# Sending ScalarE's transfers through SyncE, with longer portions of other work ahead of the gate chain's last two steps

## The chip, the cores and the metric

The kernel runs on one core of a Trainium2 chip. The metric is device time in microseconds (us). The kernel before has a median of 1401.21 us over 3 runs (1399.54 to 1405.23).

## The reference

It is one step of a two-layer trunk with 128 context tokens and 512 latent tokens of 1024 features, all in float32. Each layer normalises and modulates its input and projects it once; three branches read that projection: A, latent attention; B, differential attention; C, an mLSTM in both directions. Each branch is multiplied by its own gate path, one output projection follows, and a gated residual is added. Cut to what matters here:

```python
def mixer_layer(x, mod, l, W, rope, ctx):
    shift, scale, gate = jnp.split(mod, 3, axis=-1)
    h = rmsnorm(x, W['g_norm'][l]) * (1 + scale) + shift
    proj = h @ W['W_in'][l]
    ...
    gts = (mg + W['ml_gate_b'][l].reshape(N_ML_GATES)).astype(f32)      # input and forget gates, per token
    ...                                                                 # lf = log_sigmoid(forget), cumulated per chunk
    m_t = jnp.maximum(g, jnp.max(d, axis=-1))                           # running-max stabiliser of the scan
    ...
    y = jnp.concatenate([o_a * jax.nn.silu(z_a), o_b * jax.nn.silu(z_b), o_c * jax.nn.silu(z_c)]) @ W['W_out'][l]
    return x + gate * y, side
```

The outputs are both residual streams after a final norm and, for the context tokens, the keys, values and mLSTM states of each layer.

## The kernel before

All 640 tokens are held together as five tiles of 128. Every projection is made from three float32r products per 128 features (`mm3`, L287 to L290), because weights and activations are split in a high and a low part. A token-major unit (`tm_unit`, L478) takes 24 such matmuls of up to 256 columns per token tile; a feature-major unit (`fm_unit`, L467) takes 24 matmuls of 320 columns per half of the tokens.

Weights come through `load_w` (L263): SyncE issues the load into one of three raw slots (L278; L275 for four-dimensional sources), ScalarE casts it to the high part (L279), and VectorE or every third time GpSimd subtracts to get the low part (L282). There are five slots each for the high and the low parts.

Two mechanisms set the order of the work.

The first is written by hand. `Feed` (L80) holds the independent units of a layer in the order `ORDER` (L133): va0 qk0 mo0 zc0 qk1 gt0 and so on. A dependent chain is a generator which yields a number of us after each of its steps; `along` (L117) hands that number to `pull` (L107), which adds it to a debt and emits units while the debt is above zero, each unit taking its own number off (2.6 for a token tile, 3.2 for a feature-major half). `need` (L113) emits all that stands ahead of a named unit at once, without touching the debt.

The second is the framework's planner. It keeps the program's order as a priority, but in each engine's queue it puts what its own estimate says is ready first. Each queue is then executed in that order: an instruction whose inputs are not there holds up everything behind it on its engine. An issue of a transfer is an instruction of its engine's queue like any other.

The gate chain (`gates`, L621) stands at the head of each layer's work, after the values va0. It transposes the gate pre-activations, forms the log-sigmoid, cumulates it per chunk (L643, L644), runs the max scans (L651 to L657) and adds (L660). It then sends the stabilisers to DRAM (L663) and the prompt's final ones to the output (L665, L666), and yields 6.4. The next step takes the chunk ends (L671 to L678), forms the factors (L681 to L686), and yields 3. The last step broadcasts those factors by a matmul (`abp`, L690), transposes the result of L678 (`pa`, L696) and the stabilisers (`pb`, L697), and copies them out as columns (L700 to L702). The first mLSTM head follows (`mlstm_head`, L707): it reloads the stabilisers on all partitions (`mb`, L715), transposes keys (`pk`, L724), weights them (`kw`, L727), and computes `pst` (L732) and the state updates `cu` (L737).

Transfers that ScalarE issues in this kernel are: the stabilisers and two small outputs (L663 to L666, eight in all), the bias row of each residual gate (L369, eight) and the gate row to DRAM (L371, eight; L377 reads it back on all partitions), the new residual after a part of the output projection (L540, 60), the same in the last head of the first layer (L562, 10), and the final gain (L1217, 2). All others are issued by SyncE.

In `out_proj` (L522) a token tile's old residual is loaded (L531), VectorE multiplies the product by the gate (L538), GpSimd adds (L539) and ScalarE issues the store (L540). The gate rows (`grw`, L368) come from a ring of eight slots (`et`, L175), which also serves the exponentials of the mLSTM head (L755, L762) and its state outputs (L748). Other lines named below: L581 copies the values va out of PSUM; L595 does the same with a tanh for the output gates mo; L828 copies transposed probabilities out of PSUM; L1028 and L1030 split the latent keys; L813 and L816 split the keys of branch B; L849 and L867 store its values and keys.

Of the kernel before, what the change touches and what calls it, by code (L numbers as in the profile page):

```python
# [32 lines left out]
# columns of the constant array  # L33
C_ID, C_SEL, C_BLK, C_ONE, C_PRM, C_RC, C_RS, C_MF, C_END = (
    0, 128, 130, 138, 266, 436, 692, 948, 1204)
# columns of the parameters among them
# [29 lines left out]
def parameter_columns(I):  # L66
    """Vectors of the inputs laid out as columns of 128, and the gate biases and stabilisers on their gate rows."""
    names = ("c", "c_ctx", "g_norm", "mla_q_norm", "mla_kv_norm", "diff_norm", "ml_conv", "ml_norm",
             "state_mlstm_n", "b_mod")
    c = np.zeros((P, C_RC - C_PRM), np.float32)  # L70
    c[:, 0:R_GB] = np.concatenate([I[n].reshape(-1, P) for n in names]).T
    for d in range(2):
        for ty in range(2):
            q0 = ty * 64 + d * 32
            c[q0:q0 + H, R_GB:R_GB + DEPTH] = I["ml_gate_b"][:, d, ty, :].T
        c[d * 32:d * 32 + H, R_M0:R_M0 + DEPTH] = I["state_mlstm_m"][0, :, d, :].T
    return c


class Feed:  # L80
    """Independent work, emitted in portions between the steps of a dependent chain."""
# [41 lines left out]
def tile_hybrid(ctx: ExitStack, tc: tile.TileContext, I: dict, O: dict):  # L123
# [8 lines left out]
    # independent work of a layer, in the order in which it fills the gaps of the dependent chains  # L132
# [7 lines left out]
    class Fixed:  # L140
        """One tile from which all that stays in its place is cut."""
# [14 lines left out]
    class Ring:  # L156
        """Slots used in turn, for tiles that live for a short stretch of the program."""
# [32 lines left out]
    # ---------------------------------------------------------------- constants and parameters  # L190
# [12 lines left out]
    # silu(cond) as stationary columns: [c_hi, ctx_hi, c_lo, ctx_lo] per k  # L203
# [13 lines left out]
    # half conv weights; norm gains with the half of z's silu  # L217
# [29 lines left out]
    # ---------------------------------------------------------------- helpers  # L247
    def rsq(ss, n, mul, eps=EPS):
        """1/sqrt(ss*mul + eps) on [P, n] columns."""
        a, r = st("rqa"), st("rqr")  # L250
        V.tensor_scalar(a[:, :n], ss, mul, eps, op0=ALU.mult, op1=ALU.add)  # L251
        G.tensor_tensor(r[:, :n], a[:, :n], mhalf[:, :n], op=ALU.pow)  # L252
        return r[:, :n]
# [9 lines left out]
    def load_w(parts, kt, w, pool=3):  # L263
        """Streams a weight section; returns per-k views of its exact high and low parts."""
# [27 lines left out]
    # ---------------------------------------------------------------- modulation  # L292
# [4 lines left out]
    def mod_rows(l, c0, pool):  # L297
        ps = pj("modp")
        if pool is None:
            # before there is other work for the tensor engine: unsplit  # L300
# [34 lines left out]
    def mod_col(l, part, s, res, pool=3):  # L335
        """Columns [P, k, which] of two feature tiles of the shift or of the scale."""
# [13 lines left out]
    def mod_end(l, res, k=slice(0, 8)):  # L350
        """(1 + scale) * g and shift."""
# [11 lines left out]
    def mod_gate(l, s, pool=3):  # L363
# [5 lines left out]
        A.dma_start(out=row[0:2, :], in_=I["b_mod"][l, 2048 + s * 256:2304 + s * 256].unsqueeze(0).to_broadcast([2, 256]))  # L369
        V.tensor_tensor(row[0:2, :], ps[0:2, 0:256], row[0:2, :], op=ALU.add)  # L370
        A.dma_start(out=grow[l][:, s * 256:(s + 1) * 256], in_=row[0:2, :])  # L371

    def gate_tile(l, hf):
        """The residual gates of half of the features for the sample and for the prompt, on all partitions."""
# [5 lines left out]
    # ---------------------------------------------------------------- residual stream  # L380
# [48 lines left out]
    def norm_sample(s, xs, mods, hT):  # L429
        """Two feature tiles of the normalised sample: transposed, modulated and split."""  # L430
# [8 lines left out]
    def norm_prompt(s, xs, mods, hT):  # L439
        """Four feature tiles of the normalised prompt."""  # L440
# [16 lines left out]
    # ---------------------------------------------------------------- projections  # L457
# [9 lines left out]
    def fm_unit(hT, wv, c0, cb):  # L467
        """Feature-major unit of 128 columns: cb(half, psum of 320 tokens)."""
# [9 lines left out]
    def tm_unit(hT, wv, w, cb):  # L478
        """Token-major unit: cb(token tile, psum [P, w])."""
# [8 lines left out]
    def z_sec(l, hT, key, c0, res, h):  # L488
        """2 * silu(z) of a head, feature-major."""
# [10 lines left out]
    def head_norm(tok, sq, mul):  # L500
        """rmsnorm over the 128 features of each of the 5 token tiles; in place."""
# [7 lines left out]
    def finish(tok, tmp, gcol, z):  # L509
        """Token-major head output -> gated, feature-major, split in high and low."""  # L510
# [11 lines left out]
    def out_proj(l, br, ks, res, key, v):  # L522
        """x += gate * (heads ks of a branch) @ W_out, for all tokens."""
        for hf in range(2):
# [3 lines left out]
            for t in range(NT):  # L528
# [11 lines left out]
                A.dma_start(out=xd[v][t][:, cs], in_=xt)  # L540
                yield 0.65 * len(ks)

    def out_tail(l, br, ks, res, key, v):
        """The last heads of a layer, token tile by token tile; gives the new residual tiles."""
# [3 lines left out]
        def tile_(t):  # L548
            w = 0 if t < 4 else 1
            xs = x_tiles(v - 1, t)  # L550
            for hf in range(2):
# [9 lines left out]
                if l + 1 < DEPTH:  # L561
                    A.dma_start(out=xd[v][t][:, cs], in_=xs[hf])  # L562
# [3 lines left out]
    # ---------------------------------------------------------------- branch C: mLSTM  # L566
    def sec_va(l, hT, p, res):
        """Values of a pair of heads (and the gates with the first pair), token-major."""
# [35 lines left out]
    def conv_unit(l, hT, wv, c0, ch, res, key):  # L604
        """Depthwise conv and silu, feature-major."""
# [15 lines left out]
    def gates(l, res):  # L621
# [40 lines left out]
        for d in range(2):  # L662
            A.dma_start(out=msc[d * 4:d * 4 + 4, :], in_=m[d * 32:d * 32 + 4, :])  # L663
        # final stabilisers of the prompt
        A.dma_start(out=O["new_mlstm_m"][0, l, 0, :].unsqueeze(1), in_=mt[0:4, 639:640])  # L665
        A.dma_start(out=O["new_mlstm_m"][0, l, 1, :].unsqueeze(1), in_=mt[32:36, 512:513])  # L666
        yield 6.4
# [20 lines left out]
        yield 3  # L688
# [18 lines left out]
    def mlstm_head(l, h, res, feed, nfin):  # L707
# [8 lines left out]
        # value of [C | n] at the start of each chunk  # L716
# [33 lines left out]
        for c in range(NT):  # L750
            if c < 4:
                # q scaled by the weight of the incoming state
# [34 lines left out]
    # ---------------------------------------------------------------- attention pieces  # L787
    def rope(dst, x, t, s, on=None):
        """dst, x: [P, s*64] of sample token tile t."""
# [9 lines left out]
    def q_stack(ps, r0, n):  # L799
        """rows r0..r0+64 of ps -> [q_hi; q_lo], for each of r0."""  # L800
# [7 lines left out]
    def k_stack(ps, parts):  # L808
        """(r0, n0, kh, kl): rows r0..r0+64 of ps from column n0 -> [k_hi; k_hi], [k_lo; k_lo]."""
# [11 lines left out]
    def attend(pe, t, v3, vp, hs):  # L821
        """psum [q, dv] = P @ V, P token-major."""
# [12 lines left out]
    # ---------------------------------------------------------------- branch B: differential attention  # L835
    def sec_dv(l, hT, p, res):
        """Values of a pair of heads: sample | context cache, and prompt."""
# [16 lines left out]
    def sec_dqk(l, hT, h, res):  # L854
        """q | k of a head, token-major, rotated; the context cache as fifth key tile."""
# [100 lines left out]
    # ---------------------------------------------------------------- branch A: latent attention  # L956
# [24 lines left out]
    def mla_prep(l, res):  # L981
        ch = [*res["cq", 0], *res["cq", 1], res["cq", 2][0]]
        kr3 = res["cq", 2][1]
        # per-token norms of cq and ckv
# [16 lines left out]
        # prompt outputs  # L1001
# [8 lines left out]
        # transposed, with the gain; split  # L1010
# [4 lines left out]
        for k in range(2):  # L1015
            # columns: sample | context cache | prompt
# [29 lines left out]
        # shared rotary key: sample (rotated) | context cache | prompt  # L1046
# [13 lines left out]
        # rotary queries, token-major over all heads  # L1060
# [21 lines left out]
    def mla_v(l, p, res):  # L1082
        """Values of a pair of heads, token-major: sample | context cache, and prompt."""
# [17 lines left out]
    def mla_qk(l, h, res):  # L1101
        """Queries and keys of a head without the rotary part, feature-major, split."""
# [30 lines left out]
    def mla_head(l, h, res, feed, tail=None):  # L1133
# [45 lines left out]
        # the last head: every token tile goes on to the end of the layer by itself  # L1179
# [30 lines left out]
    # ---------------------------------------------------------------- the trunk  # L1210
    gfin = [None]

    def final_norm(t, xs):
        if gfin[0] is None:
            gfin[0] = [qt("gfin", n=512) for _ in range(2)]
            for i in range(2):
                A.dma_start(out=gfin[0][i],  # L1217
# [147 lines left out]
```

## Time and profile before

| what | value |
|---|---|
| median of 3 runs | 1401.21 us |
| runs | 1399.54, 1401.21, 1405.23 us |
| span of the profiled execution | 1399.6 us |
| PE busy | 1310.0 us, 94% |
| VectorE busy | 842.5 us, 60% |
| ScalarE busy | 630.2 us, 45% |
| GpSimd busy | 385.5 us, 28% |
| mean granted TensorE clock | 0.977 |

The span runs from the first to the last instruction. Of the profiled execution no other time is shown, so the span stands for it; it is 1.6 us below the median of the runs and equals the fastest of them. PE is TensorE's matmuls, PEld its weight loads, DVE VectorE, ACT ScalarE, POOL GpSimd. SPq and ACTq are the queues of SyncE and ScalarE when they issue transfers. A granted clock of 1.00 is 2.4 GHz, 0.50 is 1.2 GHz.

### The profile page before, as it was taken

The page shows a single profiled execution, that of the slowest core. Times are in us where ns is not written, and L with a number is a line of the kernel's source. Part 1 is how long each engine was busy: PE and PEld are TensorE (multiplying, and loading weights), DVE is VectorE, ACT ScalarE, POOL GpSimd, SP SyncE. Part 2 cuts the span into 40 slices and gives each one's busy share as a digit, 9 for nine tenths or more (in the row PEclk, how much of TensorE's full clock was granted, in tenths as well). Part 3 has the DMA queues.
Part 4 walks back from the last instruction along what each step waited for, and adds up shares of the span by engine and source line. Part 5 has one row for each costly group of instructions (what it writes and reads, how often), then busy time and mean ns, then how long its engine had stood idle before and what let it go on. Part 6 is the DMA issues. An engine that isn't in the chain of part 4 may idle for free.

```text
span 1399.6 us, 24039 instructions
## 1 busy us (share of the span) xinstructions
PE 1310.0 (94%) x9300; PEld 1218.9 (87%) x9300; DVE 842.5 (60%) x1786; ACT 630.2 (45%) x1333; POOL 385.5 (28%) x335
## 2 busy tenths in 40 slices
PE   8989999989899999999979899999999999899995
PEld 3789899969899999798769899998799999878984
DVE  2576757765567465854465767675655646385446
ACT  5454544433455545255365345443343445435433
POOL 0421422323223013511432213333322202161142
PEclk9999999999999999999989999999999999999998
DMA  9423323264223223531751333434521211242154
GB/s 341 116 83 101 111 84 112 85 212 136 81 83 111 61 62 113 167 109 54 238 176 31 84 112 86 117 82 129 180 84 57 74 46 63 87 138 85 54 173 150
DMA packets 164642, 156.40 MB, mean 112 GB/s; under 512 B 14193, under 2 KB 130593, under 8 KB 164529
## 3 DMA queue, kind: packets, MB, share of 16 engines
q1 hardware_dynamic: 154032, 135.92, 32.0%
q10 hardware_dynamic: 10496, 18.95, 3.6%
q8 instruction: 73, 1.20, 0.3%
q14 instruction: 41, 0.33, 0.1%
HBM read 131.38 MB, written 23.46 MB: 111 GB/s over the span
## 4 chain that ended last, share of the span: by engine, by line
PE 73%; DVE 12%; DMA 5%; ACT 4%; issue 2%; POOL 2%; SPq 1%; DVEq 0%; ACTq 0%; POOLq 0%
PE tm L288 8%; PE tm L289 8%; PE tm L290 8%; PE fm L288 6%; PE fm L290 6%; PE fm L289 6%; PE po L831 5%; PE op L288 2%; PE pT L826 2%; PE op L289 2%; PE op L290 2%; DVE fixr L282 1%; PE nd L767 1%; PE ds L921 1%; DVE ksl L816 1%
## 5 line engine op out<-in xcount | busy, mean ns | idle before, releaser
L288 PE MATMUL tm<-fixr 128*128 128x256 f32 (+2 forms) x1040 | 302.0, 291 | 12.4 <-DVE kp L816 4.8
L289 PE MATMUL tm<-fixr 128*128 128x256 f32 (+2 forms) x1040 | 299.4, 288 | 0.2 <-DVE fixr L282 0.2
L290 PE MATMUL tm<-fixr 128*128 128x256 f32 (+2 forms) x1040 | 297.0, 287 | 2.5 <-DVE fixr L427 2.2
L282 POOL TENSOR_TENSOR fixr<-fix,fixr 128x1024 fp32r<-128x1024 f32 (+4 forms) x51 | 121.4, 2380 | 385.0 <-ACT fixr L279 365.4
L279 ACT CAST fixr<-fix 128x1024 fp32r<-128x1024 f32 (+2 forms) x154 | 157.8, 1030 | 128.7 <-PE fm L289 38.4
L288 PEld LDWEIGHTS tm<-fixr 128*128 128x128 f32 x1040 | 201.0, 193 | 15.3 <-issue 4.7
L290 PEld LDWEIGHTS tm<-fixr 128*128 128x128 f32 x1040 | 200.3, 193 | 3.0 <-DVE fixr L427 2.4
L289 PEld LDWEIGHTS tm<-fixr 128*128 128x128 f32 x1040 | 201.0, 193 | 1.4 <-issue 0.9
L288 PE MATMUL fm<-fixr 128*128 128x320 f32 x640 | 201.3, 314 | 0.5 <-ACT od L940 0.5
L290 PE MATMUL fm<-fixr 128*128 128x320 f32 x640 | 199.3, 311 | 0.0
L289 PE MATMUL fm<-fixr 128*128 128x320 f32 x640 | 198.6, 310 | 0.0
L282 DVE TENSOR_TENSOR fixr<-fix,fixr 128x1024 fp32r<-128x1024 f32 (+3 forms) x103 | 141.6, 1377 | 66.8 <-ACT fixr L279 62.3
L288 PEld LDWEIGHTS fm<-fixr 128*128 128x128 f32 x640 | 120.3, 188 | 2.2 <-ACT od L940 0.8
L290 PEld LDWEIGHTS fm<-fixr 128*128 128x128 f32 x640 | 120.2, 188 | 0.9 <-issue 0.9
L289 PEld LDWEIGHTS fm<-fixr 128*128 128x128 f32 x640 | 120.4, 188 | 0.0
L539 POOL TENSOR_TENSOR xp<-xp,ytmp 128x512 f32<-128x512 f32 x60 | 79.1, 1329 | 107.7 <-DVE ytmp L538 58.4
L288 PE MATMUL op<-fixr,oTh 128*128 128x512 f32 x240 | 100.5, 419 | 2.9 <-ACT oTh L516 1.7
L289 PE MATMUL op<-fixr,oTh 128*128 128x512 f32 x240 | 96.7, 403 | 0.0
L290 PE MATMUL op<-fixr,oTl 128*128 128x512 f32 x240 | 95.0, 403 | 0.0
L929 ACT ACTIVATE P<-ds,fix 128x640 f32<-128x640 f32 (+1 forms) x80 | 56.7, 709 | 72.7 <-DVE fix L928 70.4
L927 DVE TENSOR_REDUCE fix<-ds 128x1 f32<-128x640 f32 (+1 forms) x80 | 56.8, 713 | 47.4 <-PE ds L922 31.0
L252 POOL TENSOR_TENSOR fix<-fix 128x5 f32<-128x5 f32 (+1 forms) x31 | 31.6, 1019 | 130.4 <-DVE fix L251 129.9
(325 smaller groups left out, 2722.2 us busy)
## 6 DMA issues: line engine op xcount, KB each, us to landing
fix<-in_W_in SPq DMA_DIRECT2D x56, 512.0 KB, 4.2
fix<-in_W_mod SPq DMA_DIRECT2D x35, 512.0 KB, 4.3
fix<-in_W_in SPq DMA_DIRECT2D x64, 256.0 KB, 3.3
xd<-xp ACTq DMA_DIRECT2D x60, 256.0 KB, 2.5
xp<-xd SPq DMA_DIRECT2D x50, 256.0 KB, 4.4
fix<-in_W_out SPq DMA_DIRECT2D x24, 512.0 KB, 5.0
gate<-grow SPq DMA_DIRECT2D x32, 256.0 KB, 5.0
wm<-in_W_mod SPq DMA_DIRECT2D x26, 256.0 KB, 5.9
```

The source lines that it names most:

```text
L252: G.tensor_tensor(r[:, :n], a[:, :n], mhalf[:, :n], op=ALU.pow)
L279: A.copy(hv, rv)
L282: e.tensor_tensor(lv, rv, hv.bitcast(F32), op=ALU.subtract)
L288: T.matmul(ps, lhsT=wh, rhs=xh, start=start, stop=False)
L289: T.matmul(ps, lhsT=wh, rhs=xl, start=False, stop=False)
L290: T.matmul(ps, lhsT=wl, rhs=xh, start=False, stop=stop)
L539: G.tensor_tensor(xt, xt, y, op=ALU.add)
L767: T.matmul(nd[:, d, 0:129], lhsT=e[:, d], rhs=va[:, c, :], start=True, stop=(c == 4))
L826: T.transpose(ps[:, c * P:(c + 1) * P], pe[:, c * P:(c + 1) * P], idt)
L831: T.matmul(po[:, 0:P], lhsT=pt[:, c * P:(c + 1) * P], rhs=v3[:, c] if t < 4 else vp[:, hs], start=(c == 0), stop=(c == n - 1))
L927: V.tensor_reduce(sc[:, m:m + 1], pv, axis=ax, op=ALU.max, negate=True)
L929: A.activation(ev, pv, AF.Exp, scale=DIFF_SCALE, bias=sc[:, 2 + m:3 + m], accum_out=sc[:, 4 + m:5 + m])
```

## The change

All transfers that ScalarE issued are issued by SyncE, and two yields of the gate chain are larger: 9 for 6.4 and 6 for 3. Nothing of the arithmetic changes. Comments and docstrings are gone too, with the lines kept.

```diff
 def mod_gate(l, s, pool=3):
-        A.dma_start(out=row[0:2, :], in_=I["b_mod"][l, 2048 + s * 256:2304 + s * 256]...)
+        nc.sync.dma_start(out=row[0:2, :], in_=I["b_mod"][l, 2048 + s * 256:2304 + s * 256]...)
         V.tensor_tensor(row[0:2, :], ps[0:2, 0:256], row[0:2, :], op=ALU.add)
-        A.dma_start(out=grow[l][:, s * 256:(s + 1) * 256], in_=row[0:2, :])
+        nc.sync.dma_start(out=grow[l][:, s * 256:(s + 1) * 256], in_=row[0:2, :])
 def out_proj(l, br, ks, res, key, v):
-                A.dma_start(out=xd[v][t][:, cs], in_=xt)
+                nc.sync.dma_start(out=xd[v][t][:, cs], in_=xt)
 def out_tail(l, br, ks, res, key, v):
-                    A.dma_start(out=xd[v][t][:, cs], in_=xs[hf])
+                    nc.sync.dma_start(out=xd[v][t][:, cs], in_=xs[hf])
 def gates(l, res):
-            A.dma_start(out=msc[d * 4:d * 4 + 4, :], in_=m[d * 32:d * 32 + 4, :])
+            nc.sync.dma_start(out=msc[d * 4:d * 4 + 4, :], in_=m[d * 32:d * 32 + 4, :])
-        A.dma_start(out=O["new_mlstm_m"][0, l, 0, :].unsqueeze(1), in_=mt[0:4, 639:640])
-        A.dma_start(out=O["new_mlstm_m"][0, l, 1, :].unsqueeze(1), in_=mt[32:36, 512:513])
-        yield 6.4
+        nc.sync.dma_start(out=O["new_mlstm_m"][0, l, 0, :].unsqueeze(1), in_=mt[0:4, 639:640])
+        nc.sync.dma_start(out=O["new_mlstm_m"][0, l, 1, :].unsqueeze(1), in_=mt[32:36, 512:513])
+        yield 9
         ...
         V.tensor_tensor(rb[:, 1], bc(blk.unsqueeze(2), [64, 8, 5]), ...)
-        yield 3
+        yield 6
         psb = sm("abp")
 def final_norm(t, xs):
-                A.dma_start(out=gfin[0][i], ...)
+                nc.sync.dma_start(out=gfin[0][i], ...)
```

## Rows read from the trace of the kernel before

**Rows 1.** The page: span, and busy time by engine.

```profile
span 1399.6 us, 24039 instructions
PE 1310.0 (94%) x9300; PEld 1218.9 (87%) x9300; DVE 842.5 (60%) x1786; ACT 630.2 (45%) x1333; POOL 385.5 (28%) x335
```

**Rows 2.** PE's waits over the span: us in total, times, longest.

```profile
PE pa L696 <- DVE gta L678: 7.4, 2, 3.7
...
PE tm L289 <- DVE fixr L282: 0.2, 1, 0.2
```

**Rows 3.** Windows around `pa`: length; PE, PEld, DVE, ACT, POOL busy (instructions), clock, DMA.

```profile
91.80:95.50 3.70, 0.01 (x1) 0.01 (x1) 3.53 (x11) 1.54 (x5) 0.00 (x0) 1.00 0.30 83
95.50:98.90 3.40, 3.40 (x16) 3.40 (x17) 1.55 (x7) 0.85 (x4) 0.46 (x1) 0.50 0.58 148
...
780.00:783.60 3.60, 0.00 (x0) 0.00 (x0) 3.46 (x12) 0.74 (x1) 0.00 (x0) 1.00 0.86 242
785.00:791.80 6.80, 6.80 (x34) 6.46 (x34) 2.32 (x5) 5.54 (x17) 4.55 (x10) 0.50 0.06 17
```

**Rows 4.** Windows of PE's `tm` matmuls after `pa`: length, busy (count), clock, DMA.

```profile
95.50:102.70 7.20, 5.62 (x35) 0.77 0.27 70
...
783.60:791.90 8.30, 6.66 (x32) 0.59 0.21 55
```

**Rows 5.** Timeline of PE, token-major unit ahead of `pa`: start, us, what.

```profile
91.28 0.28 PE L289 MATMUL tm<-fixr 128*128 128x256 f32 x1
91.40 0.28 PE L290 MATMUL tm<-fixr 128*128 128x256 f32 x1
```

**Rows 6.** Chain that ended last, piece by piece, in a feature-major unit: start, us.

```profile
755.32 0.15 PE fm L288
```

**Rows 7.** Timeline, first layer, from `pa` into the first head.

```profile
97.24 0.32 ACT L701 ACTIVATE fix<-pa 128x180 f32<-128x180 f32 x1 [0.99 <-DVE fix L700]
...
102.65 0.71 PE L724 MATMUL pk<-fix,cvt 128*128 128x128 f32 x5
103.40 1.56 DVE L727 TENSOR_TENSOR kw<-pk,fix 128x640 f32<-128x640 f32 x2
...
107.83 0.83 PE L737 MATMUL cu<-va,kw 128*128 128x129 f32 x6
```

**Rows 8.** ScalarE's waits over the span: us in total, times, longest.

```profile
ACT fixr L279 <- POOL xp L539: 8.6, 1, 8.6
...
ACT mo L595 <- DVE gm L657: 8.1, 1, 8.1
...
ACT PT L828 <- POOL xp L539: 5.2, 1, 5.2
```

**Rows 9.** PE's waits in three stretches: 560 to 592, 680 to 695, 1216 to 1250.

```profile
PE cqT L1038 <- DVE fixr L1030: 0.9, 1, 0.9
...
PE po L831 <- ACT PT L828: 1.0, 1, 1.0
...
PE cqT L1038 <- DVE fixr L1030: 1.1, 1, 1.1
```

**Rows 10.** The waits of SyncE's queue over the span: us in total, times, longest.

```profile
SPq L278 <- DVE fixr L282: 270.9, 46, 16.3
SPq L278 <- POOL fixr L282: 208.9, 36, 24.4
SPq L867 <- ACT qkp L866: 88.3, 8, 16.1
```

**Rows 11.** Transfers issued: what, queue, count, KB each, median us to landing.

```profile
xd<-xp ACTq DMA_DIRECT2D x60, 256.0 KB, 2.5
xp<-xd SPq DMA_DIRECT2D x50, 256.0 KB, 4.4
```

**Rows 12.** A store whose landing held ScalarE (timeline), and PE's wait there (165 to 175).

```profile
170.74 0.69 ACT L762 ACTIVATE fix<-mb,fix 128x128 f32<-128x128 f32 x2 [2.18 <-DMA out_new_mlstm_C<-fix]
...
PE tm L288 <- ACT va L581: 2.4, 1, 2.4
```

More of the change, by code (lines that the diff above doesn't have):

```diff
@@ L368, in mod_gate @@
         row = et("grw")
-        A.dma_start(out=row[0:2, :], in_=I["b_mod"][l, 2048 + s * 256:2304 + s * 256].unsqueeze(0).to_broadcast([2, 256]))
+        nc.sync.dma_start(out=row[0:2, :], in_=I["b_mod"][l, 2048 + s * 256:2304 + s * 256].unsqueeze(0).to_broadcast([2, 256]))
         V.tensor_tensor(row[0:2, :], ps[0:2, 0:256], row[0:2, :], op=ALU.add)
-        A.dma_start(out=grow[l][:, s * 256:(s + 1) * 256], in_=row[0:2, :])
+        nc.sync.dma_start(out=grow[l][:, s * 256:(s + 1) * 256], in_=row[0:2, :])
     def gate_tile(l, hf):
@@ L1216, in final_norm @@
             for i in range(2):
-                A.dma_start(out=gfin[0][i],
+                nc.sync.dma_start(out=gfin[0][i],
                             in_=I["g_final"][i * 512:(i + 1) * 512].unsqueeze(0).to_broadcast([P, 512]))
```

## Prediction

> **What bounds the kernel now.** I read the busy shares first: PE is busy for 1310.0 of 1399.6 us, ScalarE for 45% of the span and VectorE for 60% [rows 1]. So PE's stream of matmuls sets the time, and a change gains only where PE stands still or runs at the lower clock. Next come PE's own waits. Two long ones are `pa` (L696) waiting for L678: 7.4 us, 3.7 us in each layer. Weights are not what PE waits for: a single wait for L282, 0.2 us [rows 2]. Then I cut windows around `pa`. PE does nothing in 91.8 to 95.5 and in 780.0 to 783.6 while VectorE is busy nearly throughout, so VectorE's chain is what ends last there. Behind each gap stands a stretch at a granted clock of 0.50 instead of 1.00, 1.2 GHz instead of 2.4: 3.4 us in the first layer and 6.8 us in the second [rows 3]. Last I read who holds ScalarE. Several of its waits end with GpSimd's residual add or with the max scan, which the waiting instruction does not need; the transfer queued ahead of it does [rows 8].
>
> **The longer portions.** The debts of `Feed` can be followed by hand. Before, the pulls 3, 5, 3, 6.4 and 3 take the four halves of qk0 (3.2 each) and three token tiles of mo0 (2.6 each) ahead of the last step, and the debt ends at -0.2; the pull of 3 after it then takes token tiles four and five. That is what the trace has: 35 matmuls of `tm` come behind `pa` in the first layer and 32 in the second [rows 4]; the planner had fitted in the other 13 and 16 of the 48 of those two tiles while it expected `pa` to be late. With 9 and 6 the pulls take all five token tiles and then the first half of zc0, and the debt ends at -3.0; the pull of 3 behind `pa` then brings it to 0 and takes nothing. The second layer starts its gates with the same debt, 0, and goes the same way.
>
> So 35 (32) matmuls of `tm` and 24 of `fm` move ahead of `pa`. Successive `tm` matmuls start 0.12 us apart [rows 5], and a piece of `fm` is 0.15 us [rows 6]: 35 x 0.12 + 24 x 0.15 = 7.8 us in the first layer, 32 x 0.12 + 3.6 = 7.4 us in the second. The gaps are 3.7 and 3.7 us, so they are covered with some 4 us to spare. The moved units bring nothing of their own that is late: their weights are loaded and split in an order that PE hardly ever waits for [rows 2], and their ScalarE and VectorE parts are queued behind the chain. Removed are the two waits, 7.4 us, and half of each stretch at 0.50, 1.7 + 3.4 = 5.1 us, if the lower clock goes with the idle time that stands before it: 12.5 us. From below the gain is nothing (first rival); above 12.5 us I see none.
>
> The work is not created, it is taken from later. All units up to dqk1 come some two units earlier, their loads on SyncE's queue and their casts too. In the first head of branch B, `need` (L944) emits what is missing up to dqk1 in one lump: by the same count 13.0 us in the first layer and 7.8 in the second. The extra 5.6 us comes out of these lumps, and behind them the order is the old one. A lump is plain matmuls and hides no chain, so I cost its shrinking at nothing; if the lump were needed, it would cost the 5.6 us per layer.
>
> What is late next: nothing stands between `pa` and `pk` any more, so `kw` must be ready for `cu`. Before, `pa` began at 95.50, L701 ended 2.1 us later, and `kw` took 1.56 us from the end of `pk`. From the start of `pk` to the start of `cu` PE had 5.2 us of other work, a `fm` half among it [rows 7]. This half stays there (zc0's second). Of the 7.2 us from `pa` to `pk`, 5.6 were `tm` [rows 4]; `pk` now comes 1.6 us behind the start of `pa`, so `kw` is done near 1.6 + 0.75 + 1.6 = 4.0 us behind it and `cu` starts at 6.8. It fits, with under 3 us to spare.
>
> **The moved transfers, what they free.** 96 issues of about 0.33 us leave ScalarE, some 31 us. That is worth nothing directly, as ScalarE is busy for 45% of the span [rows 1]. What counts is the holding: ScalarE stood 8.6, 8.1 and 5.2 us in its longest holds [rows 8]. Yet PE waited little for it. Its waits in the stretches with such holds, on copies that ScalarE makes or that VectorE makes from them, are 0.9, 1.0 and 1.1 us [rows 9], together 3.0. I take 3.0. From below it is 0; from above it is the holds of 8.6 and 5.2 us themselves, 13.8. The 8.1 us hold stands at the gate chain, where PE had PSUM slots left until `pa` stopped it.
>
> **The moved transfers, what they cost.** SyncE gets 96 more instructions that wait for their producers, and behind each stand the weight loads (L278), the residual loads (L531) and the gates (L377); the casts on ScalarE and the adds on GpSimd wait for those. SyncE is held by stores today: 88.3 us in eight holds at L867, up to 16.1 us [rows 10], and PE waited 0.2 us for weights. So from below the cost is 0. From above it is one hold as long as the longest, 16.1 us, that reaches PE. The nearest row of a transfer that cost PE something is a store whose landing held ScalarE and through it PE for 2.4 us [rows 12]; I take one such, 2.4 us. The stabilisers, small outputs, L562's stores and the final gain go with this: their waits are on SyncE's own following loads or on nothing.
>
> The planner orders every queue anew, and other gaps of PE will move. One gap of 2.4 us [rows 12] more or less in each layer is my allowance, 5 us either way.
>
> **Sum.** -12.5 - 3.0 + 2.4 = -13.1 us on the span of 1399.6: 1386.5. The median of the runs is 1.6 us above that span, so I expect 1388.
>
> One place where the Trainium skill speaks against the change. A 256 KB store on ScalarE's queue landed in 2.5 us, and a load of the same size on SyncE's in 4.4 us [rows 11]. The Trainium skill, in DMA: Bandwidth & Descriptors, section Queues, rings and completion order, says that SyncE and ScalarE each own a row of rings on the same 16 engines and that an engine takes packets in turn from the rows with work. By that rule a store alone in its row is served between the loads, and on SyncE's row it stands behind them; the trace agrees as far as the two medians go. What that would do here is the fourth rival.
>
> **Rivals.**
>
> First, the gap stays, at `pa` or one step later. The planner may still put `pa` where its own estimate has it ready, or VectorE may be late for `kw`, with under 3 us to spare. For it speaks that the planner put `pa` into the middle of a tile, so its estimate of the chain is short; against it that the units now come first in the program. Then 12.5 us are not gained: 1400.
>
> Second, and slower: SyncE's order holds VectorE. The bias row of a gate (L369) is no longer issued by ScalarE but stands behind weight loads that wait for a raw slot: (270.9 + 208.9) / 82 = 5.9 us each [rows 10]. Its add (L370) stands in VectorE's queue, and everything behind it waits, the evacuation of PSUM for PE among it. Eight such rows, met halfway into a wait on average: 8 x 2.9 = 23 us, 1411. It cancels the gain from 1.6 us per row, and makes the kernel slower by over 0.5% from 2.5. Against it: the bias needs nothing but a slot, so the planner can put it far ahead.
>
> Third, ScalarE's holds cost PE more than its waits show. With the holds of 8.6 and 5.2 us in place of 1.0 [rows 8, 9]: 12.8 us less, 1375.
>
> Fourth, stores land later on the loads' ring and keep their slots. Eight gate rows to DRAM, each costing PE 2.4 us as in [rows 12]: 19 us, 1407.
>
> **Chances.** Forecast 0.52 (its own range 1380 to 1396), first rival 0.18, second 0.12, third 0.10, fourth 0.08. About 0.5%, 7 us, is what a measurement can tell from no change. Faster than 1394: 0.47 of the forecast's and the third rival, 0.57. Within: the rest of the forecast's, most of the first and the fourth, 0.28. Slower than 1408: 0.15. The range 1374 to 1407 leaves out the second rival and the outer parts of the third and fourth, some 0.18.
>
> **What would show it.** Right: no wait of `pa` among PE's waits, a granted clock of 1.00 around it, some 59 more matmuls between the scans and `pa`, no wait of ScalarE that ends with L539 or L657, PE's waits for L282 still near 0. Wrong: a wait at `pa` or `cu` of some 3.7 us (first rival), a wait of VectorE at L370 that ends with the bias (second), waits of ScalarE for a landing of `grow` (fourth).

## The result, and the profile after

The changed kernel takes 1412.87 us in the median (1411.38 to 1417.34), beside 1400.93 for the kernel before on the same chip: a ratio of 1.008, 95% interval 1.0057 to 1.0102. It is slower by 0.8%. The forecast was 1388 us and the range 1374 to 1407, so both missed; the chance given to "slower" was 0.15.

The page of the kernel after, span and busy time by engine:

```profile
span 1410.9 us, 24094 instructions
PE 1316.5 (93%) x9300; PEld 1221.3 (87%) x9300; DVE 833.8 (59%) x1786; ACT 629.3 (45%) x1333; POOL 386.2 (27%) x335
```

The span is 11.3 us longer than in [rows 1], on the same 9300 matmuls, and PE's busy time grew by 6.5 us: some of the loss stands in PE's waits, and some in matmuls that ran at the lower clock.

The stretch of the gate chain did what was forecast. PE's windows around the two places where the gaps were (length; PE, PEld, DVE, ACT, POOL busy, clock, DMA):

```profile
91.50:95.50 4.00, 4.00 (x36) 4.00 (x36) 3.83 (x12) 0.74 (x1) 0.00 (x0) 1.00 0.05 14
95.50:99.50 4.00, 4.00 (x29) 3.81 (x28) 3.06 (x6) 3.12 (x10) 0.00 (x0) 1.00 0.00 0
...
780.00:784.00 4.00, 4.00 (x36) 4.00 (x35) 3.94 (x9) 0.00 (x0) 0.00 (x0) 1.00 0.46 121
784.00:791.00 7.00, 6.22 (x42) 5.43 (x41) 3.97 (x11) 4.24 (x11) 2.38 (x1) 1.00 0.24 63
```

Beside [rows 3]: PE is busy through both, the clock is 1.00 where it was 0.50, and no wait of `pa` is left. Other waits have come, over the whole span (us in total, times, longest):

```profile
PE op L288 <- DVE ytmp L538: 12.0, 5, 3.6
...
PE krT L1055 <- POOL krr L797: 2.9, 1, 2.9
...
PE cu L737 <- DVE cs L738: 2.7, 4, 1.5
...
PE cf L743 <- DVE cs L738: 2.3, 1, 2.3
...
PE nd L767 <- DVE cs L738: 1.7, 1, 1.7
...
PE tm L289 <- DVE fixr L282: 0.2, 1, 0.2
```

In the kernel before, `op` waited 0.2 us for L538 and `krT` for L797 1.3 us. Weights are still not what PE waits for (last row, as in [rows 2]). The new waits stand in two places: in the mLSTM heads (`cu`, `cf`, `nd` wait for VectorE's state update, L738) and where a residual update runs beside attention (`op`, `krT`).

Where the time goes is best seen at equal work. I gave each matmul its median spacing in the trace of before, and read when each kernel had done a given amount of this work; the table has the difference from before in us (minus is ahead). The columns behind the first are experiments of the next section: e1 has the new portions alone, e2 the moved transfers alone, f4 the later order without the gain at the gates, f1 the portions with their work given back; e3, g1, h1 and h2 mix these. All of it is worked out from one profiled execution of each kernel, and executions differ by a few us: the profiled one of g1 took 2.2 us less than its median, that of e1 2.7 us less. The verdicts rest on the medians, the table only says where.

```
work done (us), place        after    e1    e3    f4    f1    e2    h2    g1    h1
 60  ahead of the gates       -0.1  -0.8   0.0  +0.2  +0.1  -0.4  -0.1  -0.2  -0.2
 85  gates, layer 1 over      -4.1  -4.8  -4.0  +0.1  -4.0  +0.8  +1.0  -4.2  -4.3
140  in its second head       -4.6  -5.4  -4.6  -0.4  -3.9  +0.8  +1.0  -4.1  -4.2
260  its mLSTM heads over     +2.1  +3.4  +0.4  +3.9  -3.9  +2.5  +2.6  -4.2  -4.5
360  behind the lump          -3.8  -3.9  -6.3  -1.7  -4.1  +3.1  +3.1  -4.1  -4.1
600  krT over                 +1.0  -1.0  -4.9  +1.5  -2.4  +5.7  +7.3  -2.0  -1.8
700  ahead of the gates       +1.7  -3.5  -5.7  +0.9  +1.4  +5.0  +7.2  -2.3  -1.8
760  layer 2, second head     -2.7  -7.9 -10.0  +0.9  -2.9  +4.7  +7.3  -6.6  -6.1
880  its mLSTM heads over     +2.3  -1.3  -2.4  +7.6  -2.7  +5.0  +7.6  -6.6  -5.7
1000 beside branch B          +6.0  -0.9  +1.2 +11.2  -2.5  +5.9  +9.6  -6.8  -5.2
1220 last attention           +9.6  +4.2  +6.8 +16.6  -1.0  +5.4  +9.0  -3.9  -6.0
1260 end                     +12.0  +4.3  +7.0 +16.7  -1.0  +9.3  +9.1  -0.3  -6.0
```

The kernel after gains 4.0 us at the first layer's gates and 4.4 at the second's, loses 6.7 and 5.0 in the mLSTM heads behind them, gets 5.9 back by the place behind the first layer's lump, and loses 4.8 by `krT`, 3.7 where out_proj runs beside branch B, 3.6 up to the last attention and 2.4 in it. The columns part these losses. The one in the last attention stands only where the residual stores are on SyncE and the gate loads too (after 2.4, e2 3.9, g1 3.6; 0.2 or less in the others). Those beside branch B and up to the last attention stand in f4 as well (3.6 and 5.4), where no transfer was moved. So do most of the waits of `op`; in e1, with the portions alone, over the whole span and then in two windows behind its two longest (both at a granted clock of 1.00):

```profile
PE op L288 <- DVE ytmp L538: 7.8, 4, 3.0
...
1000.10:1004.00 3.90, 3.88 (x20) 3.35 (x21) 1.36 (x4) 0.00 (x0) 1.69 (x1) 1.00 0.42 145
1023.40:1027.00 3.60, 3.55 (x18) 3.03 (x19) 1.34 (x4) 0.46 (x2) 2.55 (x2) 1.00 0.81 281
```

With the transfers alone (e2) `op` waits 4.4 us in all, with the portions given back (f1) 1.2.

### The profile page after: what moved, and what is told of

Same layout as the page of the kernel before. It is cut to its first block, busy times and chain, and to the rows that moved or that the text cites. A ratio compares the mean times of both kernels' runs of the same rounds, so it can differ in the third digit from the quotient of the medians.

```text
span 1410.9 us, 24094 instructions
## 1 busy us (share of the span) xinstructions
PE 1316.5 (93%) x9300; PEld 1221.3 (87%) x9300; DVE 833.8 (59%) x1786; ACT 629.3 (45%) x1333; POOL 386.2 (27%) x335
## 5 line engine op out<-in xcount | busy, mean ns | idle before, releaser
L282 POOL TENSOR_TENSOR fixr<-fix,fixr 128x1024 fp32r<-128x1024 f32 (+4 forms) x51 | 122.0, 2392 | 341.8 <-ACT fixr L279 341.7
L279 ACT CAST fixr<-fix 128x1024 fp32r<-128x1024 f32 (+2 forms) x154 | 157.5, 1030 | 121.2 <-PE tm L290 44.4
L288 PEld LDWEIGHTS tm<-fixr 128*128 128x128 f32 x1040 | 198.5, 191 | 6.3 <-issue 2.0
L290 PEld LDWEIGHTS tm<-fixr 128*128 128x128 f32 x1040 | 197.5, 190 | 4.2 <-DVE fixr L427 2.4
L289 PEld LDWEIGHTS tm<-fixr 128*128 128x128 f32 x1040 | 198.4, 191 | 0.9 <-issue 0.4
L282 DVE TENSOR_TENSOR fixr<-fix,fixr 128x1024 fp32r<-128x1024 f32 (+3 forms) x103 | 140.7, 1368 | 61.7 <-ACT fixr L279 57.1
L539 POOL TENSOR_TENSOR xp<-xp,ytmp 128x512 f32<-128x512 f32 x60 | 80.5, 1350 | 139.4 <-DVE ytmp L538 54.5
L929 ACT ACTIVATE P<-ds,fix 128x640 f32<-128x640 f32 (+1 forms) x80 | 56.7, 709 | 69.1 <-DVE fix L928 65.6
```

Of the source, the lines that this page charges most:

```text
L279: A.copy(hv, rv)
L282: e.tensor_tensor(lv, rv, hv.bitcast(F32), op=ALU.subtract)
L288: T.matmul(ps, lhsT=wh, rhs=xh, start=start, stop=False)
L289: T.matmul(ps, lhsT=wh, rhs=xl, start=False, stop=False)
L290: T.matmul(ps, lhsT=wl, rhs=xh, start=False, stop=stop)
L539: G.tensor_tensor(xt, xt, y, op=ALU.add)
```

## The experiments

My theory after this reading had two causes. The portions gain at the gates and lose in the heads, because the order there is moved by two units; and the transfers on SyncE cost a few us. The first four kernels split the change.

**e1_portions**: the portions alone.

```
-        yield 6.4          # behind the stores of the stabilisers
+        yield 9
-        yield 3            # ahead of pa
+        yield 6
```

> Only the two longer portions (9 and 6); every transfer stays where it was before. Theory A (the loss comes from transfers queued on SyncE): PE loses its two waits at pa and the low clock behind them, as in the changed kernel, where PE was 5.4 us and 4.4 us ahead at equal work behind the two gate chains; nothing else is lost, so 1401 - 10 = 1391 us. Theory B (the loss comes from the other work being pulled forward, so that it meets the chains at worse places): the waits at pa are gone all the same, but the losses behind them come too, 1405 to 1413 us.

1408.29 us, ratio 1.0041 (1.0024 to 1.0058). The portions by themselves lose, though the gates gain 4.0 and 4.4 us in its trace. (The 5.4 us of the expectation was read at 80 us of work, where the kernel after had not yet run `pa`.)

**e2_sync**: the transfers alone; the eight lines with `A.dma_start` that the change touches become `nc.sync.dma_start`.

> Only the issuing engine: all transfers of ScalarE on SyncE, portions as before (6.4 and 3). Theory A: the waits at pa stay, and the losses of the changed kernel come on top: it lost some 22 us (12 us slower although 10 us were won at the gates), so 1401 + 22 = 1423 us. Theory B: SyncE's queue costs nothing, 1396 to 1402 us.

1409.32 us, 1.0049 (1.0032 to 1.0067). They lose by themselves too. 0.41% and 0.49% add up to 0.9%, and the change lost 0.8%: two causes, each worth about half of the net loss.

**e3_sync_no_resid** and **e4_sync_resid_only**: the new portions, with the transfers split.

```
 e3:  L369 L371 L663 L665 L666 L1217 on SyncE; L540 L562 stay on ScalarE
 e4:  L540 L562 on SyncE; the others stay on ScalarE
```

> The changed kernel, except that the stores of the residual (L540, L562) stay on ScalarE. Theory A in the form that the residual stores are what blocks SyncE (its queue waited 162.5 us at L540 for the adds): 1391 to 1394 us, no wait of PE at op for VectorE's ytmp. If instead the gates' rows and the stabilisers block: 1405 to 1413 us. Theory B: 1405 to 1413 us.

> The longer portions, and of the transfers only the residual's stores (L540, L562) on SyncE; the gates' rows, stabilisers and the final gain stay on ScalarE. Theory A in the form of the residual stores: as slow as the changed kernel, 1409 to 1414 us, with gate and residual loads late behind them. If the gates' rows and the stabilisers block instead: 1391 to 1394 us.

e3: 1407.81 us, 1.0041 (1.0026 to 1.0056), the same as the portions alone: with the new portions, gate rows, stabilisers, small outputs and the final gain cost nothing that shows on SyncE. e4: 1412.3 us, 1.0062 (1.0038 to 1.0087); the interval takes in e1's 1.0041 and the whole change's 1.008, but beside e3's zero it points to the residual stores.

The next four went at the portions' loss and tried another issuer.

**f1_give_back**: the new portions on the old queues, and the 5.6 us of work that they pull ahead of the gates are taken out of the five pulls of the first mLSTM head.

```
-            yield 4.8
+            yield 4.8 if h else 3.68      # 5 x 1.12 = 5.6
```

> The longer portions alone (9 and 6, transfers as before), and the 5.6 us that they take are given back in the first mLSTM head: its five chunk steps yield 3.68 instead of 4.8, so that from the second head on the other work stands where it stood before. Theory C (the portions win 10 us at the gates and lose it again in the mLSTM heads, because the other work comes two units early there and meets the chain's steps at other places): the waits of cu, cf and nd in the heads go, with the low clock behind them, and the win stays, 1391 to 1395 us. Theory D (any new order costs what chance brings; the portions' loss has no place of its own): 1402 to 1412 us.

**f4_shift_only**: the kernel before, with 5.6 us more work pulled just ahead of the first head's state products, behind the gates. The heads get the shift, the gates gain nothing.

```
-        yield 3
+        yield 3 if h else 8.6
```

> The kernel before, with the 5.6 us of other work pulled not at the gates but one step later, by the first mLSTM head (its first yield is 8.6 instead of 3, in both layers); gates and transfers as before. Theory C: the waits at pa stay, and behind the first head the other work stands as early as with the longer portions, so the losses in the later heads come without the win: 1401 + 12 to 16 = 1413 to 1417 us. Theory D: 1398 to 1406 us.

f1: 1400.6 us, 0.9972 (0.996 to 0.9983). f4: 1417.9 us, 1.01 (1.0081 to 1.012). With the shift alone the kernel is slower by a full per cent; with the shift taken back the portions gain, and the table has f1 flat through both layers' heads (-3.9 to -3.9, -2.9 to -2.7) where e1 loses 8.8 and 6.6 us. So the shift is the cause of what the portions lose. What it does is seen in the second layer's heads of e1, in three windows and VectorE's timeline (start, us, what):

```profile
844.00:848.00 4.00, 3.38 (x27) 3.00 (x25) 4.00 (x6) 0.51 (x3) 2.36 (x1) 1.00 0.24 71
848.00:851.60 3.60, 1.20 (x8) 0.96 (x8) 3.60 (x9) 0.66 (x1) 0.00 (x0) 1.00 0.63 181
851.60:858.40 6.80, 6.80 (x30) 5.72 (x30) 3.08 (x15) 3.69 (x13) 1.00 (x4) 0.50 0.24 68
```

```profile
841.50 1.41 DVE L615 SCALAR_TENSOR_TENSOR cvt<-up,fix,cvt 128x511 f32<-128x511 f32 x2
842.84 3.81 DVE L756 TENSOR_TENSOR fix<-fix,cvt 128x256 f32<-128x256 f32 x3
846.57 0.34 DVE L738 SCALAR_TENSOR_TENSOR cs<-cs,fix,cu 128x129 f32<-128x129 f32 x1
846.83 1.00 DVE L616 SCALAR_TENSOR_TENSOR cvt<-up,fix,cvt 128x511 f32<-128x511 f32 x2
847.75 0.59 DVE L738 SCALAR_TENSOR_TENSOR cs<-cs,fix,cu 128x129 f32<-128x129 f32 x2
...
850.80 0.85 DVE L738 SCALAR_TENSOR_TENSOR cs<-cs,fix,cu 128x129 f32<-128x129 f32 x3
```

And the same head in f1:

```profile
848.00:851.60 3.60, 3.00 (x26) 2.81 (x25) 3.60 (x5) 1.50 (x3) 2.20 (x1) 1.00 0.49 161
851.60:858.40 6.80, 6.80 (x57) 6.23 (x56) 6.31 (x21) 3.86 (x13) 1.38 (x4) 1.00 0.61 168
```

The third L756 of e1 by itself, what GpSimd did then, and in f1 the instruction that ran beside L282, one of the conv:

```profile
844.04 2.60 DVE L756 TENSOR_TENSOR fix<-fix,cvt 128x256 f32<-128x256 f32 x1
...
843.80 2.57 POOL L282 TENSOR_TENSOR fixr<-fix,fixr 128x1024 fp32r<-128x1024 f32 x1
```

```profile
847.88 2.47 DVE L615 SCALAR_TENSOR_TENSOR cvt<-up,fix,cvt 128x127 f32<-128x127 f32 x1
...
847.71 2.48 POOL L282 TENSOR_TENSOR fixr<-fix,fixr 128x1024 fp32r<-128x1024 f32 x1 [1.76 <-ACT fixr L279]
```

In e1, VectorE is full from 844 to 851.6 us. The state updates (L738), for which `cu` and then `cf` wait, stand between the conv of the unit that has come forward (L615, L616), the scaled queries (L756) and casts; the last three end at 851.65, and PE stands 2.4 of the 3.6 us ahead of that. Then it runs 6.8 us at a clock of 0.50, 30 matmuls where f1 does 57. The instruction that ran for 2.6 us beside GpSimd's L282 stands ahead of all six of these state updates in e1; in f1 the one that did stands behind four of six. The first layer has the same: stretches at 0.50 from 165.5 and 209.9 us in e1, 1.00 in f1. The waits themselves are short (`cf` 2.3 us, `cu` 0.6); the 27 matmuls missing in the 6.8 us behind them, at the 0.12 us from one to the next of [rows 5], cost about as much again.

**f2_mb_scalar**: the new portions, and the heads' stabiliser rows (L715), which come late on SyncE in the shifted order, are issued by ScalarE.

```
-            nc.sync.dma_start(out=mb[d], in_=gd["msc"]...)
+            A.dma_start(out=mb[d], in_=gd["msc"]...)
```

> The longer portions alone, and the reload of the stabilisers (mb, L715) is issued by ScalarE instead of SyncE, where it stood behind weight loads that waited for raw slots (issued at 198.9 instead of 185.9 us in the first layer's third head). Theory C in the form that the late reload is what the shift does: the wait of ScalarE for mb there and PE's waits at cu go, about 5 us, 1403 us or less. In the form that VectorE's chain is what is late: no change, 1408 us.

1410.36 us, 1.0044 (1.003 to 1.0059): no gain on e1's 1.0041, and `cf` waits 5.0 us in two waits where e1 has one of 2.3. The late rows are not the cause.

**f3_resid_gpsimd**: the change, with the residual stores issued by the engine that makes the tile.

```
-                nc.sync.dma_start(out=xd[v][t][:, cs], in_=xt)        # and L562
+                G.dma_start(out=xd[v][t][:, cs], in_=xt)
```

> The changed kernel with the residual's stores (L540, L562) issued by GpSimd, which makes most of their data itself, so that they hold neither SyncE nor ScalarE; the other moved transfers stay on SyncE. If the residual stores cost 5 us because they hold SyncE's queue, so that residual and gate loads behind them are late: 1406 to 1409 us, as with the stores on ScalarE. If what costs is that the order is planned anew or that the stores land among the loads: 1412 us or more; GpSimd's own issue time may add to it.

1405.93 us, 1.0016 (1.0001 to 1.0031), below the change's 1.008, and the two intervals don't meet: with the new portions, what SyncE costs is in these stores. But it stands below e3 too (1.0041, the stores on ScalarE; the intervals just overlap), so GpSimd as the issuer changes more than SyncE's part. And e2's trace is 2.5 us behind by the end of the first layer's heads, ahead of its first residual store at 293.8 us: without the new portions some of the loss has another source.

The next four asked whether the causes are independent, and what stands behind the stores.

**g1_after_give_back**: the change, with f1's edit.

> The changed kernel, all transfers on SyncE, with the first head's chunk portion cut to 3.68 so that the two units pulled ahead of the gates are given back in the mLSTM heads. Theory (two separate causes: the shift of the work through the mLSTM heads costs 8 to 9 us, the residual stores on SyncE 5 to 7 us): the shift's loss is gone and the stores' loss stays, ratio to before 0.997 + 0.004 to 0.005 = 1.001 to 1.002, 1403 to 1405 us. Rival A (the shift matters only as long as ScalarE issues; on SyncE the heads lose anyway through late loads): about as the changed kernel, 1.007 to 1.009. Rival B (the two are one cause: late loads only hurt because the work is shifted): 0.996 to 0.998.

1402.75 us, 1.0004 (0.9989 to 1.0018). SyncE costs 0.49% without the new portions, 0.4% with them, and 0.3% (1.0004 beside 0.9972) with the give-back: independent within the intervals, as long as ScalarE or SyncE issues the stores.

**g2_best_gpsimd**: f1, with L540 and L562 issued by GpSimd.

> The longer portions with the give-back of 3.68, ScalarE issuing as before except that the residual stores L540 and L562 are issued by GpSimd, whose add makes the tile, so that no other engine waits for it. If ScalarE's holds by these stores cost PE the 3 us that the prediction put on them: 0.994 to 0.996, 1395 to 1398. If they cost nothing (rival): as with ScalarE issuing, 0.997 (0.996 to 0.998). If GpSimd's issues and its descriptor work delay its own adds and casts: 0.999 or more.

1403.68 us, 1.0013 (0.9995 to 1.0032): a miss for the hope that this removes ScalarE's holds for nothing. GpSimd is a better issuer than SyncE and than ScalarE in f3's order, and a worse one than ScalarE here. With GpSimd as the issuer the give-back changes nothing (1.0016 and 1.0013), where it is worth 0.7% with ScalarE (e1 and f1): what an issuer costs depends on the order. (f3 and g2 also differ in the issuer of the small transfers.) Why was not followed.

**g3_resid_loads_scalar** and **g4_gates_scalar**: the change, with one kind of load taken from behind the stores.

```
 g3:  -  nc.sync.dma_start(out=xt, in_=x_src(v - 1, t)[:, cs])        +  A.dma_start(...)     # L531
 g4:  -  nc.sync.dma_start(out=gs[w], in_=grow[l][w:w + 1, ...])      +  A.dma_start(...)     # L377
```

> The changed kernel, with the residual loads L531 issued by ScalarE, so that they do not stand behind the stores L540 on SyncE. If what the held stores delay is these loads (theory): the 5 us that the stores cost come back, 1.003 to 1.005. If it is the gate rows of L377 or the weights behind the stores (rival): as the changed kernel, 1.007 to 1.009, with the waits of GpSimd at L539 for the load shorter but those of VectorE at L538 for the gates still at 15 us or more.

> The changed kernel, with the loads of the residual gates (L377) issued by ScalarE, so that they do not stand behind the stores L540 on SyncE. If the gates behind the stores are what PE pays for (VectorE at L538 waited 20.5 us for them, 5.2 before): 1.003 to 1.005. If it is the residual loads L531 (rival): as the changed kernel, 1.007 to 1.009, with VectorE's waits for the gates gone and GpSimd's for the loads still near 40 us.

g3: 1415.36 us, 1.0101 (1.0076 to 1.0125), no gain. g4: 1407.23 us, 1.0043 (1.0026 to 1.006), the level of the portions alone; its interval and the change's just touch. GpSimd's waits for the residual loads and VectorE's for the gates, first in the kernel after, then in g4:

```profile
POOL xp L539 <- DMA xp<-xd: 42.6, 12, 14.1
...
DVE ytmp L538 <- DMA gate<-grow: 20.5, 6, 5.3
```

```profile
DVE ytmp L538 <- DMA gate<-grow: 20.7, 8, 4.2
...
POOL xp L539 <- DMA xp<-xd: 25.1, 10, 5.6
```

My expectation had these the wrong way round: the gain came with shorter waits for the residual loads, and VectorE waits for the gates as long as before in total. These totals don't explain it either: in h1 below, against g1, GpSimd's waits for the residual loads are 39.7 beside 42.0 us, and the time falls all the same. Only in single places can the path be followed. The clearest is the last out_proj, in g1: SyncE's timeline, VectorE's there, and the windows.

```profile
1335.65 2.81 SPq L540 DMA_DIRECT2D xd<-xp  x3
1338.55 0.87 SPq L377 DMA_DIRECT2D gate<-grow  x2
1339.52 0.38 SPq L531 DMA_DIRECT2D xp<-xd  x1
```

```profile
1343.68 1.29 DVE L538 TENSOR_TENSOR ytmp<-op,gate 128x512 f32<-128x512 f32 x2 [5.22 <-DMA gate<-grow]
```

```profile
1340.00:1345.00 5.00, 3.14 (x18) 2.65 (x17) 1.32 (x3) 0.69 (x1) 0.00 (x0) 0.93 0.87 258
1345.00:1350.00 5.00, 5.00 (x25) 4.33 (x24) 1.08 (x4) 0.82 (x3) 3.81 (x3) 0.73 0.57 191
```

The two gate loads stand behind three stores, VectorE waits 5.22 us for them, PE is idle for 1.9 us and then at the lower clock. The table has it: g1 goes from -3.9 to -0.3. Hence two more runs.

**h1_give_back_gates**: g1 with g4's edit. **h2_sync_gates**: e2 with g4's edit.

> The changed kernel with the give-back of 3.68 and with the gate loads L377 issued by ScalarE. With the give-back alone the trace runs 6.6 to 6.9 us ahead of before from the second layer's gates to 1220 us of work and loses 3.6 of it where two gate loads stand behind three stores on SyncE. Theory (what the stores cost comes through the gate loads): the lead is kept to the end, 0.994 to 0.997, 1393 to 1398 us. Rival (another order of transfers loses as much elsewhere): 0.999 to 1.002.

> The old portions (6.4 and 3), all that ScalarE issued on SyncE, and the gate loads L377 issued by ScalarE. With the gate loads on SyncE this was 1.0049. Theory (the moved stores cost through the gate loads, and ScalarE's freed holds are worth a few us): 0.997 to 1.001. Rival (the stores on SyncE cost through the weight and residual loads behind them): 1.003 to 1.006.

h1: 1396.86 us, 0.9961 (0.9946 to 0.9976), faster than both kernels; its lead of 6.0 us is kept to the end. Its interval and f1's (0.996 to 0.9983) overlap, so it is not shown to be faster than the portions with the give-back and every transfer where it was. The place where g1 lost, in h1:

```profile
1335.33 0.85 ACTq L377 DMA_DIRECT2D gate<-grow  x2
```

```profile
1338.00:1343.00 5.00, 5.00 (x34) 4.47 (x33) 2.49 (x6) 1.15 (x3) 1.51 (x3) 1.00 0.95 356
1343.00:1348.00 5.00, 5.00 (x34) 4.41 (x33) 1.39 (x2) 1.59 (x4) 3.64 (x3) 1.00 0.74 245
```

h2: 1409.12 us, 1.0045 (1.0029 to 1.0061), no better than e2's 1.0049. The end is mended here as well (e2 loses 3.9 us there, h2 nothing), but h2 has lost 3.6 us more than e2 by then, in pieces of 1 to 3 us at `krT` and in out_proj beside branch B. So the stores cost through the gates in one place. That in the others they cost through whatever the new order puts behind them is a guess; which loads these are in each place is not settled.

## Why the prediction was wrong, point by point

**The gates: right, at two thirds of the forecast size.** Forecast -12.5 us, 5.4 in the first layer (gap 3.7, clock 1.7) and 7.1 in the second (3.7 and 3.4) [rows 3]. Measured 4.0 and 4.4, 8.4 together: little more than the two gaps of 7.4, so the clock term of 5.1 was too large in both layers. The units counted by hand with Feed's debts went where the count put them, and the first rival, a gap that stays, did not occur.

**The step that failed first: "hides no chain, so I cost its shrinking at nothing".** I looked at the lump at the end of the shift and not at the mLSTM heads that it passes through. All work from the gates to dqk1 came two units earlier, so each dependent step of the heads met another unit. The sum had nothing for it, and it cost about 14 us: e1 is 5.7 us slower by the medians though its gates give 8.4, and f4, the shift alone, is 13.9 us slower. What the shift moved was VectorE's work in the gaps: in the head shown, conv that had stood behind four of the six state updates now stood ahead of all or most of them. The loss in the heads is 8.8 and 6.6 us in e1. f4 shows it with the shift alone (+1.0%), f1 with it removed (-0.3%). The sign at the lump was wrong too: in the first layer the shifted kernels get 5.6 to 7.3 us back there (f4, the kernel after, e1), where before and f1 have a wait of PE for L496 of 3.0 us between 308 and 390 that they don't have. And "behind them the order is the old one" does not hold: matched against before, the sequence of matmuls of e1 differs in 185 places, among them some at 525 to 589 us, far behind the lump; that of f1 differs in 23, all but one pair of them at the gates and in the first heads. The waits of `op` near 1000 and 1023 us in e1 stand in this wider reordering: VectorE waits 7.5 us there for two pairs of gate loads, with no residual store on SyncE. e1's 5.1 us from 1000 to 1220 belong to it too; I have not followed them. The price that I named for the lump, 5.6 us per layer, is not far from the size of the loss, but it was tied to the wrong place and left out of the sum.

**`kw` ready before `cu`: right.** No wait of `cu` for `kw` in the kernel after; its waits are for L738.

**The freed ScalarE: the direction shown in one place.** The holds of L279 and L828 by L539 and of L595 by L657 [rows 8] are gone; one wait of 1.3 us that ends with L539 is left, at L929. In f1, where ScalarE still issues, PE loses 3.8 us in the attention around 680 to 704 us that g1 does not. f1's windows there, and ScalarE's and PE's waits in that stretch:

```profile
680.00:684.00 4.00, 2.58 (x17) 2.01 (x16) 0.27 (x1) 0.00 (x0) 1.64 (x2) 1.00 1.04 383
...
688.00:692.00 4.00, 4.00 (x20) 4.00 (x19) 1.49 (x1) 1.04 (x4) 0.57 (x1) 0.50 0.41 119
```

```profile
ACT Pa L1163 <- POOL xp L539: 6.7, 1, 6.7
```

```profile
PE pT L826 <- ACT Pa L1163: 2.0, 1, 2.0
```

ScalarE stands 6.7 us at a store that waits for GpSimd's add, PE 2.0 us for the softmax behind it, and the clock falls. Before, the same hold was 5.4 us and cost PE 0.7. So the third rival's idea (holds cost more than PE's waits show) holds in this one place. No run isolates the 3.0 us: how much of it the kernel after gained cannot be told from the rest, and g2, which takes the stores' holds off ScalarE, is slower than f1.

**The transfers on SyncE, a term that was mis-sized.** The ratios make it a loss of 0.3 to 0.5%, 4.5 to 7 us, net of what ScalarE's freedom gives back; the forecast had 2.4 - 3.0, a gain of 0.6 us. I judged by PE's waits for weights (0.2 us), and these did stay at 0.2. But SyncE also carries the loads of the residual update, and the stores that now stand among them wait for it:

```profile
SPq L540 <- POOL xp L539: 162.5, 51, 30.4
```

That is more holding than the 88.3 us of L867 in [rows 10], from which I took that SyncE can bear it. But the total does not set the loss: h1, which is faster than before, has as much.

```profile
SPq L540 <- POOL xp L539: 161.2, 55, 26.2
```

Where a gate or residual load behind such a store comes late, `op` cannot free its PSUM and PE waits. Of the 12.0 us in five waits of the kernel after, two of 2.0 us (near 683 and 1358 us) stand where e1 has none; the other three, near 1004, 1028 and 1249 us, 8.1 together, stand where e1 waits 7.8 without any residual store on SyncE, and belong to the shift. So the path to PE is shown for the last out_proj and argued for the rest of the 4.5 to 7 us.

**Second and fourth rivals: slower, but elsewhere.** The bias rows (L369) and gate rows (L371) cost nothing on SyncE (e3 as e1), and VectorE waits at L370 for the matmul only, 0.8 us in all. Nor did stores land later among the loads, as the fourth rival had it: the median is 2.2 us on SyncE's queue, beside 2.5 on ScalarE's in [rows 11]. So the 2.5 us beside the loads' 4.4 was no sign of separate rows, as the prediction read it: on one queue the two are as far apart. That does not refute the rule of the Trainium skill itself (DMA: Bandwidth & Descriptors, section Queues, rings and completion order), which no run here tests.

```profile
xd<-xp SPq DMA_DIRECT2D x60, 256.0 KB, 2.2
xp<-xd SPq DMA_DIRECT2D x50, 256.0 KB, 4.5
```

What is late is the issue, not the landing, where the path can be followed. The mechanism of the second rival, SyncE's order holding VectorE, is what the last out_proj shows, at L538 and by way of L540 instead of L369.

**The planner's allowance** of 5 us either way was a spread around zero. The one shift tried by itself (f4) lost by nearly three times as much, 13.9 us by the medians.

## What to carry to other kernels

Work pulled into one gap is taken from an order, and everything up to the place where the order is the old one again moves with it: follow each chain in that stretch, or give the same amount back right behind the gap, which here turned +0.4% into -0.3%. Before a store goes to a queue that loads share, name every load that will stand behind it and its reader; "PE does not wait for weights" says nothing of the other loads. When a change has two halves, look for each new wait in kernels that have one half alone before you put it down to either. Changes of about 0.4% that have different causes can be measured one by one, and their repairs together gave 1396.9 us (0.9961 of before) where the change gave 1412.9 (1.008).

## What the runs showed of the hardware that was not expected

A wait of PE of 2 us can stand ahead of a stretch at a granted clock of 0.50: in e1 6.8 us with the 2.3 us wait of `cf` ahead of it, in f1 a stretch that takes in 688 to 692 us with the 2.0 us wait of `pT` ahead of it. But the length of the one wait does not tell: the two waits of `op` in e1 that ended at 1000.1 and 1023.4 us, 2.9 and 3.0 us long, were followed by a clock of 1.00 (the windows above). So short waits can cost more than the waits say, and whether one does has to be read from the clock behind it.

Single VectorE instructions took several times their usual time beside GpSimd's L282. In e1 three of L756 took 0.68, 0.68 and 2.60 us; the third began 0.24 us after an L282 had and ended 0.27 us after its end. In f1's same head it was the second conv instruction of L615, 2.47 us, with its end 0.16 us after that of L282, and the L756 there took 0.43 to 0.68 us beside GpSimd's L759. It is not every instruction: in the kernel before all 18 of L764 that began during an L282 took 0.39 to 0.42 us. What decides was not tried alone.
